# Block 1's mixer computed with the matrix memory before the retention, and RWKV's two directions stepped alternately

## The chip, the cores and the metric

The kernel runs on one core of a Trainium2 chip. The metric is the device time of one execution in microseconds (us), the median of several runs. The profile is one further execution; its span is counted from the first to the last recorded instruction.

## What is computed

Two transformer blocks follow each other on a sequence of 256 tokens of width 1024. Block 1 sees 16 learned meta tokens ahead of it (272 rows):

```python
proj = einsum('bnd,dk->bnk', rmsnorm(h), w_in)          # 4112 columns
rq, rk, rv, rg, mq, mk, mv, mo, gate_pre = split(proj)  # eight of 512, one of 16
ret = retention(rotary(rq), rotary(rk), rv)             # forward + backward, 4 heads
y_ret = head_norm(ret, ret_gn_g) * silu(rg)
mq, mk = split(silu(conv5([mq, mk])))
hm = mlstm(mq, mk, mv, gates(gate_pre))                 # forward + backward, 4 heads
y_m = head_norm(sigmoid(mo) * hm, mlstm_gn_g)
h = h + concat([y_ret, y_m]) @ w_out
h = h + expert_choice_ffn(h)                            # 16 experts, capacity 34
...
```

Block 2 mixes the 256 tokens with a context of 256 more by two branches, a gated delta rule (4 heads) and RWKV-7 (8 heads, forward and backward, `S_t = S_{t-1} (diag(w_t) + a_t b_t^T) + v_t k_t^T`), merges both, and ends with 32 small experts in groups. All of it is float32.

## The kernel before, in words

One class, `Net`, builds three stages in one program. The framework below it orders the instructions of every engine itself, once, when the kernel is built: each engine then runs its own list in that order and waits by semaphores. The order of the Python statements gives the priorities, so a block that is written earlier tends to come earlier, and where buffers or banks are missing it comes later.

**`head`** (0 to about 293 us) is block 1's mixer up to the router. `head_body` (L401) loads the rows, norms and transposes them (`uT`), and multiplies by `w_in` in groups of 256 columns. `wgroup` (L378) loads one group (1 MB) into a slot of a ring of weight slots and splits it into two halves of reduced mantissa: the high part by ACT (`wp`, L289), the low part by DVE (`wp`, L290), two instructions of each for a group. `product3` (L299) makes a float32 product of three matmuls (high by high, high by low, low by high). `projT` (L451) gives a 128-column block transposed (`pj`, 24 matmuls), `projN` (L494) a group in token rows (`pn`), with the 16 meta rows by `metas` (L389; `pM`, L395). PSUM has banks under tags: `pa` three, `pc` two, `pm` two, `pb` one.

The parts stand in this order: retention's `rq` and `rk` with rotation (L457 to L475), its decayed scores `rs` times `strip` into `pret` (L484, L485), its values `rv` by `projN(1024)`, its sums `ro` and their head norm (L518 to L525), then the matrix memory: `mq` and `mk` with the convolution (`cv`, L543 and L546), the gates, `mv` by `projN(3072)`, per head the scores (`ms` L616, `pm`) and the sums `mo` (L639), each sum followed by a small chain over ACT and DVE (`rc` L642 to L644, `y` L646 and L647). Then `mo`'s projection (`projN(3584)`), the product with it on POOL (L659) and the head norm (L729 to L733), retention's gate (`pj`, then three ACT instructions L304 to L306 for a sigmoid, then `gate`, L671), and the transposes `trb` of `y` (L680) into `yT`: columns 0 to 3 are retention's (`gate` L684, split by ACT L289 and DVE L290), 4 to 7 the matrix memory's (ACT L688, DVE L689). POOL copies the meta columns of `yT` to `um` (L690). With `um` and `yT` the output product starts: `pM` (L395) and `wo` (L299), four groups of `w_out`. Between the projections `step()` (L427) issues pieces of block 2's adaptive norm (`ada`, L1037), 24 weight loads of 1 MB with 8 matmuls each, through the same ring.

**`ffn`** (about 293 to 1670 us) streams block 1's 16 experts (three matrices of 1024 x 2816) through the same ring of slots (loads by L241 and L283 on SP's queue); the context's part of block 2's mixer runs beside them. Each expert's second product is done one expert later.

**`lat`** (from 1670 us) is block 2 for the 256 tokens. `rwkv` (L1415) works on four pairs of heads, `j` = 0 to 3. For each pair and direction `d`: `rwkv_front` (L1600) builds the triangular matrices (`rmt`, L1628), `rwkv_back` (L1639) inverts them (`r0i…` and `r1i…`, L1164 and L1192, 32x32 and 128x128 matmuls), and then walks over four chunks; each walks through `rp` (L1661, L1676, L1683, L1691) and the state `rSU` (DVE and ACT at L1680, DVE at L1688, POOL `rsw` at L1672). These are generators: a helper `run` drives one to its end. While direction 0 runs, `hop` (through `fill`, L1118) puts pieces of waiting work behind its matmuls: projections `pc` (L1102), the delta rule (`gic`, `gib`, `gp`), the next pair's preparation. `rwkv_out` (L1707) merges the two directions. Direction 0 uses PSUM tag `pa`, direction 1 `pc`, two banks each. After the mixer come its merge and the 32 experts (from about 2140 us).

Of the kernel before, what the change touches and what calls it, by code (L numbers as in the profile page):

```python
# [16 lines left out]
P = 128  # L17
# [145 lines left out]
class Net:  # L163
# [237 lines left out]
    def head_body(self, W):  # L401
# [9 lines left out]
        wq = self.wgroup(w_in, 0)  # L411
# [30 lines left out]
        for hh in range(4):  # L442
            s = rvt(hh, f"strip{hh}")[:, :416] if hh < 3 else W.tile([P, 416], F32, name="strip3", tag="mv0", padded_shape=[P, 516])
# [13 lines left out]
        rqk = []  # L457
        for g in range(2):
            dst = W.tile([P, 4, NTOK], F32, name="qk", bufs=4)
            scale = (P ** -0.5) if g == 0 else 1.0  # L460
            for j in range(4):
                if j % 2 == 0:
                    w = wq if g + j == 0 else self.wgroup(w_in, 512 * g + 128 * j)
                    if g:
                        step(g)
                pj = projT(w, j % 2)
                raw = W.tile([P, NTOK], F32, name="raw", tag="raw", padded_shape=[P, NTOK + 4], bufs=3)
                nc.scalar.activation(raw, pj, AF.Copy, scale=scale)
                tmp = W.tile([P, NTOK], F32, name="rtmp", tag="rtmp", bufs=2)
                for i in (0, 64):  # L470
                    a, c = slice(i, i + 64), slice(64 - i, 128 - i)
                    nc.vector.scalar_tensor_tensor(tmp[a], pj[c], scale, self.ht("sin")[c], op0=ALU.mult, op1=ALU.mult)
                nc.gpsimd.tensor_mul(dst[:, j, :], raw, self.ht("cos"))
                nc.vector.tensor_add(dst[:, j, :], dst[:, j, :], tmp)
            rqk.append(dst)  # L475

        big = W.tile([P, 4, 3, NTOK], F32, name="pret", tag="big")
        prets = [big[:, hh] for hh in range(4)]
        self.ptag = "pc"
        for hh in range(4):  # L480
            pret = prets[hh]
            for t, (n0, n) in enumerate(TT):
                b = self.bank("rs")
                nc.tensor.matmul(b[:n, :NTOK], rqk[1][:, hh, n0:n0 + n], rqk[0][:, hh, :], start=True, stop=True)  # L484
                nc.vector.tensor_mul(pret[:n, t, :], b[:n, :NTOK], strip[hh][:n, 144 - n0:416 - n0])  # L485
# [3 lines left out]
        rv = [rvt(t, f"rv{t}") for t in range(3)]  # L489
# [24 lines left out]

        projN(1024, out_rv)


        self.ptag = "pc"  # L518
        for t, (n0, n) in enumerate(TT):
            ro = self.bank("ro")  # L520
            for hh in range(4):
                for m, (m0, mn) in enumerate(TT):
                    nc.tensor.matmul(ro[:n, hh * P:(hh + 1) * P], prets[hh][:mn, m, n0:n0 + n],
                                     rv[m][:mn, hh * P:(hh + 1) * P], start=(m == 0), stop=(m == 2))
            self.head_norm(W, y[:n, t, 0:512], ro[:n], n, f"r{t}")  # L525


        self.ptag = "pa"
        mqk = []
        for g in range(2):  # L530
            dst = W.tile([P, 4, NTOK], F32, name="qk", bufs=4)
            for j in range(4):
                if j % 2 == 0:
                    w = self.wgroup(w_in, 2048 + g * 512 + 128 * j)
                    step(1)
                pj = projT(w, j % 2)
                pad = W.tile([P, NTOK + 4], F32, name="pad", tag="raw", bufs=3)
                nc.gpsimd.memset(pad[:, 0:2], 0.0)
# [876 lines left out]
    def rwkv(self, W, F, uT, S, lat, load, tags, start=None):  # L1415
# [92 lines left out]
        for j in range(4):  # L1508
# [8 lines left out]
            for d in range(2):  # L1517
                ys.append(run(self.rwkv_back(j, d, x, fr[d], env)))
# [764 lines left out]
```

## Time and profile before

| what | value |
|---|---|
| runs, us | 2493.68, 2490.26, 2485.04 (median 2490.26) |
| profiled execution, us | 2486.04 |
| its span, us | 2484.3 |
| mean granted TensorE clock (share of full speed) | 0.965 |
| PE busy / DVE / ACT / POOL, us | 2306.2 / 990.8 / 656.0 / 350.8 |
| bytes moved by DMA, mean rate | 755.06 MB, 304 GB/s |

PE is TensorE, PEld its weight loads, DVE VectorE, ACT ScalarE, POOL GpSimd, SP the engine whose queue issues most DMAs. The span contains the three stages one after the other; an engine's share over the span therefore mixes stages with different limits, and the tables by stretches show each of them. [...]

### The profile page before, as it was taken

What the parts mean: (1) busy time and instruction counts of PE and PEld (TensorE: products, weight loads), DVE (VectorE), ACT (ScalarE), POOL (GpSimd) and SP (SyncE); (2) the same over time, 40 slices, a digit from 0 to 9 for tenths busy, and PEclk for the clock granted to TensorE, in tenths of its full rate; (3) what the DMA queues carried; (4) which work ended last, traced back from release to release, by engine and by line L of the source; (5) the groups of instructions that cost most, each with busy time, mean ns of one, the idle gap of its engine ahead of it and who ended that gap; (6) DMA issues with size and microseconds to landing.
All of it is one profiled execution on the core that took longest, in us unless ns stands there. A gap on an engine that the chain in (4) does not pass through costs nothing. (4 is left out here: it accounts for less than half of the span.)

```text
span 2484.3 us, 45165 instructions
## 1 busy us (share of the span) xinstructions
PE 2306.2 (93%) x18736; PEld 1252.2 (50%) x18736; DVE 990.8 (40%) x2419; ACT 656.0 (26%) x1652; POOL 350.8 (14%) x627
## 2 busy tenths in 40 slices
PE   7997799999999999899999998978998999989997
PEld 6765433444444434333433333327777777865554
DVE  6655311323332133223133133216566563645545
ACT  4443111211211222111122121114534332522221
POOL 3101100000001111101011011004243231300000
PEclk9998899999999999999999999998997889999999
DMA  7664999999999999999999999992311113689995
GB/s 244 225 233 132 336 407 402 402 407 405 400 407 398 361 402 405 406 408 406 406 400 406 406 406 406 408 354 67 88 37 38 45 27 95 224 278 365 367 367 182
DMA packets 318816, 755.06 MB, mean 304 GB/s; under 512 B 12944, under 2 KB 158016, under 8 KB 315536
## 3 DMA queue, kind: packets, MB, share of 16 engines
q1 hardware_dynamic: 317104, 747.67, 80.3%
q0 software_dynamic: 1504, 4.46, 0.6%
q8 instruction: 150, 2.46, 0.4%
q14 instruction: 58, 0.48, 0.1%
HBM read 751.03 MB, written 1.05 MB: 303 GB/s over the span
## 5 line engine op out<-in xcount | busy, mean ns | idle before, releaser
L901 PE MATMUL gu<-w,xs 128*64 128x512 f32 (+1 forms) x3072 | 677.2, 568 | 24.3 <-DMA w<-in_w_up 17.2
L901 PEld LDWEIGHTS gu<-w,xs 128*64 128x64 f32 x3072 | 197.5, 137 | 325.2 <-issue 258.0
L933 PE MATMUL dn<-w,hT 128*64 128x512 f32 x1408 | 338.1, 604 | 17.0 <-DMA w<-in_w_down 16.9
L1102 PE MATMUL pc<-luT,w 128*128 128x256 f32 x688 | 177.5, 398 | 1.8 <-DMA w<-in_w_in 1.8
L933 PEld LDWEIGHTS dn<-w,hT 128*64 128x64 f32 x1408 | 88.4, 136 | 171.7 <-issue 116.7
L1102 PEld LDWEIGHTS pc<-luT,w 128*128 128x128 f32 x688 | 126.6, 195 | 19.2 <-DMA w<-in_w_in 2.0
L2139 PE MATMUL egu<-w,exs 128*64 128x256 f32 x1024 | 123.2, 383 | 0.0
L2139 PEld LDWEIGHTS egu<-w,exs 128*64 128x64 f32 x1024 | 74.6, 136 | 39.4 <-issue 6.9
L1672 POOL TENSOR_SCALAR rsw<-rSU,rwc 64x64 f32<-64x64 f32 x112 | 37.2, 332 | 389.3 <-DVE rSU L1688 379.0
L911 DVE TENSOR_TENSOR hid<-hid,gu 128x512 f32<-128x512 f32 (+1 forms) x48 | 30.8, 642 | 130.8 <-ACT hid L306 130.7
L912 DVE TENSOR_TENSOR hid<-hid,gu 128x512 f32<-128x512 f32 (+1 forms) x48 | 30.8, 642 | 119.3 <-PE gu L901 119.2
L1102 PE MATMUL pc<-cuT,w 128*128 128x256 f32 x288 | 71.1, 391 | 0.0
L304 ACT ACTIVATE hid<-gu 128x512 f32<-128x512 f32 (+1 forms) x48 | 26.9, 561 | 160.9 <-PE gu L901 160.7
L2166 PE MATMUL edn<-w,ehT 128*64 128x512 f32 x256 | 67.7, 597 | 0.7 <-ACT ehT L321 0.5
L1102 PEld LDWEIGHTS pc<-cuT,w 128*128 128x128 f32 x288 | 52.0, 189 | 30.8 <-issue 20.4
L1680 DVE COPY rSU<-rp 64x64 f32<-64x64 f32 x64 | 13.8, 215 | 133.0 <-PE rp L1676 132.7
L1628 PE MATMUL rmt<-rT,rBK 128*128 128x128 f32 (+1 forms) x256 | 54.4, 355 | 13.1 <-DVE rT L1615 6.2
L289 ACT CAST wp<-w 128x1024 fp32r<-128x1024 f32 (+1 forms) x48 | 55.1, 1188 | 40.3 <-DMA w<-in_w_in 22.6
L299 PE MATMUL pj<-uTh,wp 128*128 128x272 f32 x320 | 64.8, 296 | 0.0
L290 DVE TENSOR_TENSOR wp<-w,wp 128x1024 fp32r<-128x1024 f32 (+1 forms) x44 | 57.2, 1323 | 15.0 <-ACT wp L289 15.0
L1185 DVE TENSOR_TENSOR r0iB<-r0iB,r0ic 128x128 f32<-128x128 f32 x48 | 13.7, 285 | 114.2 <-PE r0ic L1164 107.4
L2182 DVE TENSOR_TENSOR acc<-acc,esc 128x512 f32<-128x512 f32 x64 | 41.0, 682 | 42.5 <-PE esc L2181 42.5
(675 smaller groups left out, 3560.1 us busy)
## 6 DMA issues: line engine op xcount, KB each, us to landing
w<-in_w_down SPq DMA_DIRECT2D x176, 1024.0 KB, 16.8
w<-in_w_gate SPq DMA_DIRECT2D x128, 1024.0 KB, 17.7
w<-in_w_up SPq DMA_DIRECT2D x128, 1024.0 KB, 17.5
w<-in_w_gate SPq DMA_DIRECT2D x64, 768.0 KB, 16.1
w<-in_w_up SPq DMA_DIRECT2D x64, 768.0 KB, 14.8
w<-in_moe_w_gate SPq DMA_DIRECT2D x32, 1024.0 KB, 13.2
w<-in_moe_w_up SPq DMA_DIRECT2D x32, 1024.0 KB, 12.2
w<-in_moe_w_down SPq DMA_DIRECT2D x32, 1024.0 KB, 11.3
```

Of the source, the lines that this page charges most:

```text
L289: self.nc.scalar.copy(hi, src)
L290: (eng or self.nc.vector).tensor_sub(lo, src, hi)
L299: self.nc.tensor.matmul(out, a[x], b[y], start=(i == 0 and x + y == 0), stop=(i == n - 1 and x == 1))
L901: ins = nc.tensor.matmul(b[h * 64:(h + 1) * 64, :w], xs[:, k, :], ws(k, slice(h * w, (h + 1) * w)), start=(k == 0), stop=(k == KD - 1))
L911: nc.vector.tensor_mul(hid, hid, gu[0][:, :w])
L933: ins = nc.tensor.matmul(dn[0][dc * 64:(dc + 1) * 64], hT[:, j, h * 64:(h + 1) * 64], wd(h * nf + j, slice(dc * 512, (dc + 1) * 512)), sta ...
L1102: self.nc.tensor.matmul(b, w(k), uT[:, k, :], start=(k == 0), stop=(k == KD - 1))
L1628: ins = nc.tensor.matmul(b[:, i], BK[:, c0 + i, h:h + 2, :], T[:, h, c0 + i, :, :], start=True, stop=True)
L1672: nc.gpsimd.tensor_scalar(sw[r], SU[r, h, c, :], wc[r, c:c + 1], 0.0, op0=ALU.mult, op1=ALU.add)
L2139: nc.tensor.matmul(b[64 * i:64 * i + 64, x * 256:x * 256 + 256], xs[:, k, i, :], w[i](k), start=(k == 0), stop=(k == KD - 1))
L2166: nc.tensor.matmul(b[64 * i:64 * i + 64, :], hT[:, j, 64 * i:64 * i + 64], wd[i](j, cs), start=(j == 0), stop=(j == 1))
L2182: nc.vector.tensor_add(h[:, t, cs], h[:, t, cs], b)
```

## The change

Three edits. In `head_body` the matrix memory's projection, gates, values, scores and sums now stand first, then retention's, then `mo`'s projection, the head norm of the matrix memory and retention's gate. The first weight group is that of `mq`; the fourth `strip` has a buffer of its own, and the tiles `rv`, which share buffers with the first three strips, are taken after the scores `pret`. The eight column blocks of `y` are transposed in the order 4 to 7, 0 to 3. In `rwkv` the two directions' `rwkv_back` are driven by `in_turn`, one step of each in turn, where they were driven one after the other; the fills still hang on direction 0 alone.

```diff
-        wq = self.wgroup(w_in, 0)
+        wq = self.wgroup(w_in, 2048)
...
-            s = rvt(hh, f"strip{hh}")[:, :416] if hh < 3 else W.tile([P, 416], F32, name="strip3", tag="mv0", padded_shape=[P, 516])
+            s = rvt(hh, f"strip{hh}")[:, :416] if hh < 3 else W.tile([P, 416], F32, name="strip3")
...
-        rqk = []
-        for g in range(2):
...
-                    w = wq if g + j == 0 else self.wgroup(w_in, 512 * g + 128 * j)
-                    if g:
-                        step(g)
...
-                nc.vector.tensor_mul(pret[:n, t, :], b[:n, :NTOK], strip[hh][:n, 144 - n0:416 - n0])
...
-        projN(1024, out_rv)
...
-            self.head_norm(W, y[:n, t, 0:512], ro[:n], n, f"r{t}")
...
         mqk = []
...
-                    w = self.wgroup(w_in, 2048 + g * 512 + 128 * j)
-                    step(1)
+                    w = wq if g + j == 0 else self.wgroup(w_in, 2048 + g * 512 + 128 * j)
+                    if g:
+                        step(1)
...
         sums(3, pm)
+        self.ptag = "pa"
+        rqk = []
+        for g in range(2):
...
+                    w = self.wgroup(w_in, 512 * g + 128 * j)
+                    step(1)
...
+                nc.vector.tensor_mul(pret[:n, t, :], b[:n, :NTOK], strip[hh][:n, 144 - n0:416 - n0])
+
+        rv.extend(rvt(t, f"rv{t}") for t in range(3))
+        projN(1024, out_rv)
...
+            self.head_norm(W, y[:n, t, 0:512], ro[:n], n, f"r{t}")
...
         mo = [rvt(t, f"mo{t}") for t in range(3)]
         projN(3584, out_mo)
...
-        for k in range(KD):
+        for k in (4, 5, 6, 7, 0, 1, 2, 3):
             b = self.bank("trb")
...
-            ys = []
-            for d in range(2):
-                ys.append(run(self.rwkv_back(j, d, x, fr[d], env)))
+            ys = self.in_turn(tags, [self.rwkv_back(j, d, x, fr[d], env) for d in range(2)])
...
+    def in_turn(self, tags, gens):
+
+        out = [None] * len(gens)
+        todo = list(range(len(gens)))
+        while todo:
+            for i in list(todo):
+                self.ptag = tags[i]
+                try:
+                    next(gens[i])
+                except StopIteration as end:
+                    out[i] = end.value
+                    todo.remove(i)
+        return out
```

What the framework makes of it is seen in the engines' lists. **PE, the last sums of the matrix memory** (`mo<-mv,pm`; `trb<-ctab,y` are the transposes of `y`, `pM` and `wo` the output product). Before, they are the last thing ahead of the transposes and the output:

```order
L639 MATMUL mo<-mv_568,pm_1644 128x129
L639 MATMUL mo<-mv_568,pm_1648 128x129
L680 MATMUL trb<-ctab,y 128x16 x3
L680 MATMUL trb<-ctab,y 128x128 x6
L680 MATMUL trb<-ctab,y 128x16
L680 MATMUL trb<-ctab,y 128x128 x2
L395 MATMUL pM<-w,um 32x256 x8
L299 MATMUL wo<-wp,yT_2124 128x256 x2
```

Now, retention's scores (`rs`) and its value projection (`pn`) come behind them:

```order
L597 MATMUL mo<-mv_584,pm_1010 128x129
L597 MATMUL mo<-mv_584,pm_1014 128x129
L641 MATMUL rs<-qk 16x272
L641 MATMUL rs<-qk 128x272 x2
L641 MATMUL rs<-qk 16x272
L641 MATMUL rs<-qk 128x272
L299 MATMUL pn<-wp,uTh 128x256 x2
L299 MATMUL pn<-wp,uTl 128x256
```

The twelve sums each of the last two heads stand directly ahead of these, with nothing but one small `pM` among them. The line numbers of the changed file are other ones: L597 is the sum, L641 the score, L682 the transpose.

**DVE, the end of the head** (`gate<-pj` is the product behind the last sigmoid, `wp<-w` the split of `w_out`, `hM<-hM,pM` belongs to the output product already). Before:

```order
L729 BN_STATS hnst<-y 128x6 x4
L730 BN_AGGR hnmv<-hnst 128x2 x4
L729 BN_STATS hnst<-y 128x6 x4
L730 BN_AGGR hnmv<-hnst 128x2
L733 TENSOR_SCALAR y<-y,hnmv 128x128 x4
L730 BN_AGGR hnmv<-hnst 128x2 x3
L733 TENSOR_SCALAR y<-y,hnmv 128x128 x4
L689 SCALAR_TENSOR_TENSOR yT_2125<-trb,pcol,yT_2124 128x272 x4
L713 TENSOR_TENSOR hM<-hM,pM 16x256
```

Now:

```order
L735 TENSOR_SCALAR y<-y,hnmv 128x128 x4
L673 SCALAR_TENSOR_TENSOR gate<-pj,pcol,gate 128x272
L691 SCALAR_TENSOR_TENSOR yT_2125<-trb,pcol,yT_2124 128x272 x3
L686 TENSOR_TENSOR gate<-trb,gate 128x272 x2
L290 TENSOR_TENSOR wp<-w,wp 128x1024
L686 TENSOR_TENSOR gate<-trb,gate 128x272 x2
L290 TENSOR_TENSOR wp<-w,wp 128x1024
L691 SCALAR_TENSOR_TENSOR yT_2125<-trb,pcol,yT_2124 128x272
L290 TENSOR_TENSOR yT_2125<-gate,yT_2124 128x272 x4
L323 COPY arow<-ada 128x256
L290 TENSOR_TENSOR wp<-w,wp 128x1024
```

The head norm (`hnst`, `hnmv`, `y`) stands ahead of the last gate now, and behind that gate come products, splits and two of `w_out`'s low parts. On SP's queue the first load of `w_out`, which stood ahead of the load of `hM` and of the last two `ada` loads, now stands behind `hM` and the first of these two; the other three loads of `w_out` stay last.

**PE, the second chunk's step of the first pair** (`rp` is the recurrence; `rT_11729` belongs to direction 0, `rT_11730` to direction 1; `r1ic` is the inversion of direction 1, `rbw` the next pair's preparation). Before:

```order
L1661 MATMUL rp_12623<-rSU_12108,rT_11729 64x64 x2
L1164 MATMUL r1ic<-r1iB 32x32 x16
L1567 MATMUL rbw<-rlo_11679,rlora 128x256
L1567 MATMUL rbw<-rlo_11680,rlora 128x256
L1668 MATMUL rp_12623<-rSU_12108,rT_11729 64x64 x2
L1676 MATMUL rp_12634<-rP_12627,rY_12199 64x64 x2
L1164 MATMUL r1ic<-r1iZ,r1iB 32x32 x16
L1691 MATMUL rp_12623<-rSU_12108,rMR_12118 64x64
L1567 MATMUL rbw<-rlo_11679,rlora 128x256
L1567 MATMUL rbw<-rlo_11680,rlora 128x256
L1683 MATMUL rp_12634<-rSU_12108,rKt_12117 64x64 x2
L1691 MATMUL rp_12623<-rSU_12108,rMR_12118 64x64
```

Now:

```order
L1682 MATMUL rp_12819<-rSU_12108,rT_11729 64x64 x2
L1690 MATMUL rp_12838<-rP_12831,rY_12199 64x64 x2
L1675 MATMUL rp_12828<-rSU_12154,rT_11730 64x64 x2
L1705 MATMUL rp_12819<-rSU_12108,rMR_12118 64x64
L1682 MATMUL rp_12828<-rSU_12154,rT_11730 64x64 x2
L1690 MATMUL rp_12849<-rP_12842,rY_12235 64x64 x2
L1705 MATMUL rp_12828<-rSU_12154,rMR_12164 64x64
L1697 MATMUL rp_12838<-rSU_12108,rKt_12117 64x64 x2
L1705 MATMUL rp_12819<-rSU_12108,rMR_12118 64x64
L1675 MATMUL rp_12866<-rSU_12108,rT_11729 64x64 x2
L1697 MATMUL rp_12849<-rSU_12154,rKt_12163 64x64 x2
L1705 MATMUL rp_12828<-rSU_12154,rMR_12164 64x64
```

Direction 1's inversion, which stood between direction 0's matmuls, is finished before the first step, and its own steps stand there in its place.

## Rows read from the trace of the kernel before

**Rows 1.** The page, the span in 40 equal slices: busy tenths of the DMA engines.

```profile
DMA  7664999999999999999999999992311113689995
```

**Rows 2.** SP's queue, 0 to 330 us: loads waiting for a ring slot (total, times, longest).

```profile
SPq L241 <- PE pM L395: 40.1, 4, 29.7
```

**Rows 3.** The head in stretches of 10 us: busy time (x instructions) by engine, clock, DMA.

```profile
200.00:210.00 10.00, 8.18 (x54) 4.85 (x53) 6.79 (x19) 4.66 (x11) 1.10 (x2) 0.99 0.66 211
210.00:220.00 10.00, 4.70 (x16) 3.72 (x16) 5.83 (x22) 3.65 (x12) 3.36 (x4) 0.50 0.06 7
220.00:230.00 10.00, 3.33 (x16) 2.11 (x20) 7.28 (x33) 2.98 (x9) 1.93 (x3) 0.50 0.00 0
230.00:240.00 10.00, 10.00 (x82) 7.66 (x82) 1.25 (x3) 1.20 (x2) 0.00 (x0) 0.82 0.32 105
```

**Rows 4.** PE's timeline, 196 to 236 us: start, length, instructions, idle time before them.

```profile
207.24 2.40 PE L639 MATMUL mo<-mv,pm 16*128 16x129 f32 x16 [0.82 <-DVE y L647]
...
214.16 4.70 PE L639 MATMUL mo<-mv,pm 16*128 16x129 f32 x16 [4.51 <-DVE rc L643]
...
223.82 0.90 PE L680 MATMUL trb<-ctab,y 128*128 128x128 f32 x3 [2.89 <-DVE y L733]
...
229.87 1.94 PE L395 MATMUL pM<-w,um 128*32 128x256 f32 x16 [1.65 <-POOL um L690]
```

**Rows 5.** ACT's groups by line, 0 to 290 us: busy us, mean ns of one, idle before.

```profile
L646 ACT ACTIVATE y<-mo,rc 128x128 f32<-128x128 f32 (+1 forms) x12 | 4.3, 357 | 3.6 <-DVE rc L644 3.5
...
L305 ACT ACTIVATE gate<-gate,prow 128x272 f32<-128x272 f32 x4 | 2.1, 522 | 0.1
L306 ACT ACTIVATE gate<-gate 128x272 f32<-128x272 f32 x4 | 1.7, 423 | 0.0
...
L304 ACT ACTIVATE gate<-pj 128x272 f32<-128x272 f32 x4 | 1.6, 398 | 5.5 <-PE pj L299 5.5
```

**Rows 6.** DVE's groups by line, 0 to 290 us.

```profile
L290 DVE TENSOR_TENSOR wp<-w,wp 128x1024 fp32r<-128x1024 f32 x40 | 48.2, 1226 | 14.2 <-ACT wp L289 14.1
...
L647 DVE SCALAR_TENSOR_TENSOR y<-mo,rc,y 128x128 f32<-128x128 f32 (+1 forms) x12 | 4.0, 337 | 4.6 <-ACT y L646 4.1 <-ACT rc L642 0.4
...
L643 DVE TENSOR_TENSOR rc<-rc,gcol 128x2 f32<-128x2 f32 (+1 forms) x12 | 2.0, 176 | 3.2 <-ACT rc L642 3.2
L671 DVE SCALAR_TENSOR_TENSOR gate<-pj,pcol,gate 128x272 f32<-128x272 f32 x4 | 2.0, 500 | 2.1 <-ACT gate L306 2.1
...
L689 DVE SCALAR_TENSOR_TENSOR yT<-trb,pcol,yT 128x272 fp32r<-128x272 f32 x4 | 1.8, 498 | 1.1 <-ACT yT L688 1.1
L644 DVE RECIPROCAL rc<-rc 128x2 f32<-128x2 f32 (+1 forms) x12 | 1.8, 156 | 0.2
L684 DVE TENSOR_TENSOR gate<-trb,gate 128x272 f32<-128x272 f32 x4 | 1.7, 436 | 0.2 <-PE trb L680 0.2
...
L290 DVE TENSOR_TENSOR yT<-gate,yT 128x272 fp32r<-128x272 f32 x4 | 1.7, 422 | 0.5 <-ACT yT L289 0.5
```

**Rows 7.** PE's groups by line, 0 to 290 us.

```profile
L1037 PE MATMUL ada<-w,adas 128*32 128x512 f32 x192 | 28.2, 602 | 0.0
```

**Rows 8.** SP's timeline, 130 to 260 us: issue of the first w_out load.

```profile
183.53 0.38 SPq L383 DMA_DIRECT2D w<-in_w_out  x1
```

**Rows 9.** ACT's timeline, 160 to 212 us: the first cast of w_out.

```profile
189.78 1.99 ACT L289 CAST wp<-w 128x1024 fp32r<-128x1024 f32 x2 [0.90 <-DMA w<-in_w_out]
```

**Rows 10.** The latent mixer: whole, then three stretches of 10 us.

```profile
1709.00:2106.00 397.00, 363.57 (x5037) 288.27 (x5036) 237.08 (x680) 159.20 (x497) 133.91 (x240) 0.89 0.18 49
...
1790.00:1800.00 10.00, 4.68 (x91) 3.19 (x78) 9.56 (x22) 7.58 (x24) 6.26 (x7) 0.85 0.06 16
...
1890.00:1900.00 10.00, 9.13 (x61) 7.80 (x62) 7.71 (x22) 4.25 (x13) 4.99 (x11) 0.53 0.01 4
...
1910.00:1920.00 10.00, 10.00 (x212) 8.16 (x210) 2.62 (x9) 2.85 (x10) 2.07 (x6) 0.50 0.20 56
```

**Rows 11.** PE's waits in the latent mixer, 1700 to 2110 us (total, times, longest).

```profile
PE rp L1661 <- DVE rSU L1688: 11.1, 6, 4.3
```

More of the change, by code (lines that the diff above doesn't have):

```diff
@@ L455, in projT @@
             return b
-        rqk = []
+        self.ptag = "pa"
+        mqk = []
         for g in range(2):
             dst = W.tile([P, 4, NTOK], F32, name="qk", bufs=4)
-            scale = (P ** -0.5) if g == 0 else 1.0
             for j in range(4):
                 if j % 2 == 0:
-                    w = wq if g + j == 0 else self.wgroup(w_in, 512 * g + 128 * j)
+                    w = wq if g + j == 0 else self.wgroup(w_in, 2048 + g * 512 + 128 * j)
                     if g:
-                        step(g)
+                        step(1)
@@ L466, in head_body @@
                 pj = projT(w, j % 2)
[L467 to L484, printed above, removed]
-                nc.vector.tensor_mul(pret[:n, t, :], b[:n, :NTOK], strip[hh][:n, 144 - n0:416 - n0])
+                pad = W.tile([P, NTOK + 4], F32, name="pad", tag="raw", bufs=3)
@@ new lines, in head_body @@
+                nc.gpsimd.memset(pad[:, 0:2], 0.0)
+                nc.gpsimd.memset(pad[:, NTOK + 2:], 0.0)
+                nc.scalar.copy(pad[:, 2:NTOK + 2], pj)
+                c = 4 * g + j
+                tmp = W.tile([P, NTOK], F32, name="cv", tag="rtmp", bufs=2)
+                nc.vector.tensor_scalar(tmp, pad[:, 0:NTOK], self.pc("conv_w", c * 5), self.pc("conv_b", c),
+                                        op0=ALU.mult, op1=ALU.add)
+                for k in range(1, 5):
+                    nc.vector.scalar_tensor_tensor(tmp, pad[:, k:k + NTOK], self.pc("conv_w", c * 5 + k), tmp,
+                                                   op0=ALU.mult, op1=ALU.add)
@@ L488, in head_body @@
+                self.sigmoid(dst[:, j, :], tmp)
+                nc.gpsimd.tensor_mul(dst[:, j, :], dst[:, j, :], tmp)
+            mqk.append(dst)
         self.y = y = self.pers.tile([P, 3, D], F32, name="y", tag="tok")
-        rv = [rvt(t, f"rv{t}") for t in range(3)]
+        rv = []
         mv = [W.tile([P, 4, 129], F32, name=f"mv{t}") for t in range(3)]
```

57 lines of the change are left out of this document (30 added, 27 removed).

## The prediction

> **What bounds the kernel now.** I read the page's forty slices first, and there the DMA row [rows 1]. From the fifth to the twenty-seventh slice the DMA engines are at nine tenths or more: block 1's experts are bound by their weights. So are the last experts, in the slices from about 2230 us on. Between them lies a stretch with hardly any DMA, the latent mixer, and ahead of the first lies the head. Both stages that the change touches stand in front of a stream of weights, so what they gain or lose moves the stream as a whole. The waits of SP's queue bear this out at the head's end [rows 2]: the first expert loads wait four times, the longest for 29.7 us, for a ring slot that the matmuls `pM` on `w_out` free. Nothing streams in meanwhile: the DMA share is 0.06 and 0.00 from 210 to 230 us [rows 3]. The head's end is therefore the moment at which `pM` and `wo` begin. I call the idle time before it the bubble.
>
> **The bubble of before.** The table of stretches [rows 3] has PE busy 8.18, 4.70 and 3.33 us in the three tens from 200 to 230 us, which leaves 13.8 us idle. [...] From 230 to 240 us the clock is 0.82, 1.8 us more. The bubble costs 13.8 + 4.0 + 1.8 = 19.6 us. The timeline [rows 4] says what it is made of: the last sums of the matrix memory wait 4.51 us for `rc`, which stands on DVE behind two low parts of `w_out`; the transposes wait for the head norm's `y`, `pM` waits 1.65 us for `um`. Sixteen sums take 2.40 us ahead of the long wait and 4.70 behind it.
>
> **What the change does to the head.** The work is the same: no matmul, load or DVE instruction is added, so only idle time and clock can move.
>
> *The new end.* The last sums, their chain and the matrix memory's head norm now lie ahead of retention's gate and its 24-matmul projections. After the last projection comes a sigmoid on ACT, 0.398 + 0.522 + 0.423 = 1.34 us [rows 5], then DVE's list in the order shown above: `gate` 0.50, four `yT` of the matrix memory 4 x 0.498 = 1.99, four products 4 x 0.436 = 1.74, two low parts of `w_out` 2 x 1.226 = 2.45, four low parts of `yT` 4 x 0.422 = 1.69 [rows 6]. That is 8.4 us. For `um` I add 1 us: in [rows 4] 1.65 us were waited for it, of which one `yT` is 0.5. The end is 10.7 us long. Beside it PE has 24 transposes, which take 0.45 us per three at full clock (half of the 0.90 of [rows 4]), so 3.6 us, and twelve `ada` matmuls of 28.2 / 192 = 0.147 us [rows 7], 1.8 us. Idle: 10.7 - 5.4 = 5.3 us, and I add 1 for the clock. Bounds: zero, if DVE has done most of its list beside the projections; 12.6, if the first load of `w_out` comes late too. That load is now issued behind one more `ada` load. Before, it was issued at 183.53 us [rows 8] and cast from 189.78 [rows 9], 6.3 us later and long before `wo`; I take that cover as still there and cost the move at nothing, and if it is gone, at 6.3.
>
> *The new middle.* The sums of the last two heads now come back to back: six tiles through two PSUM banks. A tile frees its bank when its chain is done: sums 2.40 / 4 = 0.60 us [rows 4], then the reciprocal and the two scalings, 0.176 + 0.156 + 0.337 on DVE [rows 6] and 0.357 on ACT [rows 5], 1.6 us with no hop counted. `rs` follows in the same two banks, and the value projection `pn` behind it cannot pass, since PE takes its list in order. On DVE two pairs of low parts stand among these chains, 4 x 1.226 = 4.9 us. The nearest row is the 4.51 us that one such pair cost before [rows 4]; with two pairs I expect nearly twice this, 8 us, and 2 us of clock behind it. Bounds: 4.5 (one pair is hidden) and 16 (both at 4.5, three rounds of 1.6 for the chain, 2 of clock).
>
> The sum for the head: 19.6 - 6.3 - 10 = **3.3 us gained**; by the ends 15 gained (19.6 - 4.5) and 9 lost (19.6 - 12.6 - 16). The fourth `strip`'s own buffer, the other first weight group and the order of the transposes cost nothing by themselves; the last puts the half that is ready first, and its effect is in the list above.
>
> **What the change does to RWKV.** In the mixer, 1709 to 2106 us, PE is busy 363.6 of 397 us and its mean clock is 0.89 [rows 10]: 33 us idle, and about 0.11 x 397 = 44 us of clock. The instructions are again the same, and filling work remains behind the last pair in both versions, so a shorter chain for direction 1 is worth only the idle time it removes. PE waits six times, 11.1 us, for `rSU` of a chunk's step [rows 11]. With the two directions in turn one wait serves both chains: half of it, 5.5 us. I add 2 for a little of the clock, where the half speed follows such waits (0.53 at 1890 us). Against it: direction 1's inversion no longer stands between direction 0's steps, as the third pair of lists shows. Where DVE is full with the next pair's preparation, PE is busy 4.68 of 10 us even with that cover (1790 us, DVE 9.56) [rows 10]. Another 5.3 us idle for each of the three pairs that have a next one would be 16 us. These ends, 16 lost and 33 gained, are far apart; I take **7.5 us gained**, near the row of the six waits, since both chains now end together and the delta rule's inversions fill between most steps.
>
> [...] From 1910 to 1920 us PE is busy 10.00 of 10 us and yet granted 0.50 [rows 10]. [...]
>
> **Sum.** 3.3 + 7.5 = 10.8 us. The profiled execution took 2486.04 us, so its counterpart takes 2475. It lies 4.2 us below the median of the three runs, 2490.26, so I forecast a median of **2479 us**. About 0.3%, 7.5 us, is what a measurement of this kernel tells from no change.
>
> **The rivals.**
> 1. *Forecast* (0.47): the end gains, the middle gives back half of it, the mixer gains some. 2479, by itself 2470 to 2488.
> 2. *The stall moves, nothing is gained* (0.22). The middle costs 13 us, still under its upper bound, and takes all that the end gives (19.6 - 6.3), and the mixer's filling was as good already. For it: PE is busy 364 of 397 us there, and DVE's list has the low parts of weights between the sums' chains again, as at the end before [rows 4]. Against it: the six waits on `rSU`, which the pairing touches. 2490, 2484 to 2496. The variant that the lists are changed but the waits are the same belongs here.
> 3. *Slower: the paired steps lie bare* (0.21). Two chains that wait at the same time leave nothing between, and the next pair's front cannot begin while direction 1 still walks, as it did before. Price: the 16 us above, less 3 for the head and with 3 for a clock that drops behind the gaps: 2490 + 16 = 2506. It decides if PE's idle time in the mixer rises from 33 to over 45 us.
> 4. *The clock stays up* (0.10). If the waits behind which it fell at 1890 us go, half of the 44 us of clock comes back beside the 10.8: 2490 - 33 = 2457.
>
> **How the numbers follow.** The range leaves out the outer half of the third and fourth case: 2458 to 2505. Faster by over 0.3% (below 2483): seven tenths of the first case, all of the fourth and a little of the second, 0.33 + 0.10 + 0.03 = 0.46. Slower (above 2498): nearly all of the third and a few hundredths from the second's upper end, 0.22. Within: 0.32. Faster and slower are both open; the forecast's own range is 2470 to 2488.
>
> **What would show it.** In the changed profile: no stretch near the head's end at clock 0.50 with PE below half, and `pM` waiting at most 6 us in all behind the last gate; a new wait of PE on `rc` or `pret` in the middle of the head, 5 to 10 us, with low parts ahead of it on DVE; the first expert load some 3 us earlier than now; in the mixer, `rp` of both directions in pairs, PE's idle time about 26 us, and the six waits on `rSU` fewer. The prediction is wrong if the middle costs more than 16 us, if the mixer's idle time grows, or if the streams' start moves without the end of the kernel moving with it.

## The result, and the profile after

The changed kernel takes 2465.4 us (median of 4 runs, 2461.25 to 2467.81) against 2489.46 us of before (4 runs, 2485.04 to 2493.68): a ratio of 0.9895, 95% interval 0.9879 to 0.9911. That is 24 us faster, in the direction of the forecast and inside its range, and more than twice the 10.8 us of its sum. The profiled execution took 2467.81 us, its span is 2466.0 (before 2484.3), its mean clock 0.965, the same as before.

**The head.** The first expert load, in SP's timeline before and after:

```profile
231.87 15.30 SPq L241 DMA_DIRECT2D w<-in_w_gate  x3
```

```profile
227.04 15.32 SPq L241 DMA_DIRECT2D w<-in_w_gate  x3
```

It is issued 4.8 us earlier in this pair of profiles. Over all the profiles of the table below the gain is smaller: the load is issued between 229.7 and 231.9 us (mean 230.9) in the four profiles without any edit of the head, and between 227.0 and 230.4 us (mean 228.6) in the twelve with the head's edits, 2.3 us earlier. The bubble of [rows 3] is gone from the end and has come back smaller in two places. The table of stretches of the changed kernel (columns as in [rows 3]):

```profile
130.00:140.00 10.00, 6.28 (x37) 3.43 (x37) 4.52 (x13) 3.27 (x8) 1.09 (x2) 1.00 0.98 319
140.00:150.00 10.00, 7.45 (x27) 4.54 (x25) 4.27 (x13) 3.37 (x8) 0.00 (x0) 0.51 0.01 3
150.00:160.00 10.00, 10.00 (x51) 7.27 (x52) 3.93 (x10) 0.37 (x1) 0.00 (x0) 0.81 0.00 0
210.00:220.00 10.00, 9.52 (x65) 5.09 (x64) 7.30 (x27) 6.36 (x18) 0.00 (x0) 1.00 1.04 368
220.00:230.00 10.00, 6.92 (x48) 4.33 (x49) 8.56 (x14) 5.94 (x11) 0.46 (x1) 0.83 0.81 252
```

In the middle PE is idle 3.7 and 2.6 us in two neighbouring tens, and its clock is 0.51 in the second and 0.81 in the ten behind them; at the end it is idle 0.5 and 3.1 us at clocks of 1.00 and 0.83. Its timeline names the waits, with the columns of [rows 4]:

```profile
139.87 4.09 PE L597 MATMUL mo<-mv,pm 16*16 16x129 f32 x16 [3.72 <-DVE y L605]
...
145.98 2.38 PE L597 MATMUL mo<-mv,pm 16*128 16x129 f32 x8 [2.03 <-DVE y L605]
...
224.88 0.44 PE L1028 MATMUL ada<-ctab,arow 128*128 128x128 f32 x2 [2.11 <-DVE arow L323]
225.24 1.76 PE L395 MATMUL pM<-w,um 128*32 128x256 f32 x16
```

The sums wait for `y`, the last step of their chains, where they waited for `rc` at the end before; at the end PE waits for `arow`, the copy of the adaptive norm's row, and `pM` no longer waits at all.

**The mixer.** From its first transpose (`afT` of the tokens) to the first matmul of the merge (`mo`) the same 5372 matmul records stand. (A float32 matmul of the program stands in the trace as two records, as the added ones of e5 show, 258 records for 129 matmuls; the counts of the rows are records.) The stretch before and after (columns as in [rows 10]):

```profile
1679.61:2140.38 460.77, 425.64 (x5372) 343.16 (x5373) 264.73 (x741) 194.66 (x588) 148.40 (x278) 0.90 0.22 60
```

```profile
1676.79:2120.72 443.93, 406.89 (x5373) 332.51 (x5373) 259.13 (x741) 193.91 (x588) 149.68 (x278) 0.90 0.22 62
```

It is 16.8 us shorter, 460.8 to 443.9. It starts 2.8 us earlier and so ends 19.7 us earlier; the end of the kernel comes 18.3 us earlier. But PE's idle time did not fall: 460.8 - 425.6 = 35 us outside its matmuls before, 443.9 - 406.9 = 37 after. The clock is 0.90 in both. What fell is the time in which PE is busy, with the same matmuls. The stretch that answers to [rows 10] is as busy as before and holds 98 records more:

```profile
1709.00:2106.00 397.00, 362.62 (x5135) 293.79 (x5136) 236.96 (x688) 165.52 (x507) 132.32 (x235) 0.89 0.22 61
```

The waits for the state did shrink, but others grew by as much. Before, beside the line of [rows 11] (columns as there):

```profile
PE rp L1691 <- DVE rSU L1680: 2.7, 3, 1.3
...
PE r1ic L1164 <- DVE r1iB L1185: 0.3, 1, 0.3
```

After:

```profile
PE rp L1705 <- DVE rSU L1694: 5.9, 6, 2.3
PE rp L1675 <- DVE rSU L1702: 5.4, 4, 2.1
...
PE r1ic L1166 <- DVE r1iB L1187: 3.5, 1, 3.5
```

The six waits of a step's first matmuls fell from 11.1 to 5.4 us (four of them), those of its last matmuls rose from 2.7 to 5.9: 2.5 us less for the state in sum. One wait of direction 1's inversion rose from 0.3 to 3.5 us and took that back.

**What became cheaper.** Two places in PE's timeline of the kernel before, with equal work ahead of the second row of each:

```profile
2101.05 1.89 PE L1102 MATMUL pc<-luT,w 128*128 128x256 f32 x8
2102.88 0.68 PE L1727 MATMUL ryt<-ctab,rys 64*64 64x64 f32 x16
...
2104.26 1.89 PE L1102 MATMUL pc<-luT,w 128*128 128x256 f32 x8
2105.99 0.59 PE L1732 MATMUL rgb<-rsg,rg 128*128 128x256 f32 x2
```

Eight records `pc` of 128x256, in tiles of 128x128, occupy 1.83 us up to the next matmul if that works in tiles of 64x64 (`ryt`), and 1.73 if it has their own shape (`rgb`). Over the mixer's records the same shows as a fixed time: a 128x256 matmul is followed after 216 ns by one of its own shape and after 309 ns by a 32x32 one; a 32x32 matmul is followed by its like after 7 ns and by one of 128x128 after 121 ns (medians at full clock, the same in both kernels). The change costs something once more behind it: the first 128x256 record behind a change is followed by its own shape after 320 ns instead of 216 (median again). So the way out of the large tiles costs 93 ns, the way back some 0.1 us, and the first large matmul there another 104: about 0.3 us for two changes, 0.15 for one. In the mixer the list of before has 446 such changes and the list after has 342. Adding up every interval across a change and the one behind it, less the mean of its like at the same clock, gives 68 us before and 53 after, so 15 of the 16.8 us. What TensorE does in these 93, 114 and 104 ns no run here shows.

### The profile page after: what moved, and what is told of

The parts are those of the page before. It is cut to its first block, busy times and chain, and to the rows that moved or that the text cites. A ratio compares the mean times of both kernels' runs of the same rounds, so it can differ in the third digit from the quotient of the medians.

```text
span 2466.0 us, 45172 instructions
## 1 busy us (share of the span) xinstructions
PE 2288.3 (93%) x18736; PEld 1241.2 (50%) x18736; DVE 981.3 (40%) x2419; ACT 653.4 (26%) x1652; POOL 354.1 (14%) x627
## 5 line engine op out<-in xcount | busy, mean ns | idle before, releaser
L2196 DVE TENSOR_TENSOR acc<-acc,esc 128x512 f32<-128x512 f32 x64 | 41.0, 683 | 42.5 <-PE esc L2195 42.4
```

The lines of the kernel that those rows point to most:

```text
L2196: nc.vector.tensor_add(h[:, t, cs], h[:, t, cs], b)
```

## The experiments

Each mixer below runs from `afT` to `mo`. "Changes" are neighbours in PE's timeline there whose tile shapes differ; "idle" is PE's gaps, each counted from the end of the matmul before it, with the one ahead of the first `afT`, which lies before the stretch and is 8.5 to 8.6 us long in every profile (the stretch less its busy time is smaller by that much); "half clock" is the time there with a granted clock of 0.50.

| profile | changes | idle, us | half clock, us | mixer, us | first expert load, us | ratio to before (95%) |
|---|---|---|---|---|---|---|
| before | 446 | 43.7 | 90.1 | 460.8 | 231.9 | |
| before again (e12) | 446 | 42.7 | 113.1 | 466.8 | 229.7 | |
| change | 342 | 45.6 | 91.5 | 443.9 | 227.0 | 0.9895 (0.9879 to 0.9911) |
| change again (e9) | 342 | 44.5 | 78.2 | 437.9 | 228.7 | 0.9868 (0.9853 to 0.9884) |
| RWKV alone (e1) | 342 | 51.5 | 56.2 | 438.4 | 230.9 | 0.9904 (0.9878 to 0.993) |
| head alone (e2) | 418 | 42.4 | 74.8 | 446.8 | 228.8 | 0.9911 (0.9881 to 0.994) |
| head alone again (e14) | 418 | 42.7 | 74.7 | 447.2 | 228.8 | 0.9911 (0.9895 to 0.9928) |
| inversions in turn (e3) | 352 | 48.8 | 87.1 | 448.7 | 228.1 | 0.9927 (0.9899 to 0.9955) |
| steps in turn (e4) | 425 | 53.0 | 94.0 | 466.2 | 227.9 | 1.0019 (1.0007 to 1.0031) |
| pieces split (e5) | 559 | 48.0 | 101.4 | 497.3 | 230.2 | 1.0152 (1.0123 to 1.0181) |
| pieces joined (e6) | 429 | 45.8 | 64.9 | 464.3 | 228.3 | 1.0059 (1.0035 to 1.0083) |
| fills on second (e7) | 325 | 47.4 | 73.6 | 438.3 | 230.4 | 0.9898 (0.9872 to 0.9924) |
| larger fills (e8) | 315 | 57.0 | 81.3 | 447.3 | 228.6 | 0.993 (0.9902 to 0.9957) |
| fewest shapes (e10) | 281 | 57.7 | 112.8 | 456.2 | 228.3 | 0.9946 (0.9933 to 0.996) |
| before, lumped (e11) | 400 | 46.7 | 70.8 | 449.4 | 231.0 | 0.9949 (0.9934 to 0.9963) |
| transposes only (e13) | 433 | 42.0 | 106.0 | 458.3 | 234.0 | 0.9968 (0.9954 to 0.9982) |
| low parts on POOL (e15) | 343 | 48.3 | 69.2 | 441.3 | 227.6 | 0.9883 (0.986 to 0.9905) |

A least-squares fit over the seventeen rows gives: mixer - idle = 315 + 0.154 x changes + 0.344 x half clock (and 14 more for the two kernels with added matmuls). The errors of the two slopes are 0.007 and 0.022, and no row lies more than 2.2 us off; without the two kernels with added matmuls the slopes are 0.156 and 0.351. The comparisons below use the first two prices. Each row is one profile, and the two rows of before and of the change show how far half clock moves between profiles of one kernel (23 and 13 us).

**e1, RWKV alone.** `rwkv_back` through `in_turn`, `head_body` as before.

```diff
-                ys.append(run(self.rwkv_back(j, d, x, fr[d], env)))
+            ys = self.in_turn(tags, [self.rwkv_back(j, d, x, fr[d], env) for d in range(2)])
```

> RWKV's two directions in turn, block 1's mixer as before. Theory of tile shapes: PE pays about 0.1 us each time the tile shape changes from one matmul to the next (in both traces a 128x256 matmul is followed after 216 ns by one of its own shape and after 309 ns by a 32x32 one; from 32x32 to 128x128 it takes 121 ns instead of 7). PE's list of the latent mixer has 446 such changes in the kernel before and 342 in this one: 104 fewer at 0.11 to 0.15 us, so 12 to 16 us faster than before, with PE's idle time in the mixer unchanged (30 to 34 us). Theory of shared waits (the prediction's): at most 7.5 us faster, and by less idle time. Theory that neither edit does it alone: below 5 us.

Measured: 2464.18 us against 2490.12, 26 us faster, the whole of the gain by itself. The changes account for 104 x 0.154 = 16 us, as the theory of shapes had it; the rest comes with a half clock of 56 instead of 90 to 113 us (12 to 20 us), against 8 us more idle time, where the theory of shapes had expected none. The theory of shared waits falls: idle time rose.

**e2 and e14, the head alone.** The head's edits, with RWKV's directions one after the other.

```diff
-            ys = self.in_turn(tags, [self.rwkv_back(j, d, x, fr[d], env) for d in range(2)])
+            ys = []
+            for d in range(2):
+                ys.append(run(self.rwkv_back(j, d, x, fr[d], env)))
```

> Block 1's mixer with the matrix memory first (and the transposes in the new order), RWKV's directions one after the other as before. The first expert load comes 4 to 6 us earlier than the 231.9 us of before, by every theory. Theory of tile shapes: the list of the latent mixer, which the scheduler orders again, happens to have 418 changes of shape instead of 446, worth 3 to 4 us more: 7 to 10 us faster in all. Theory of shared waits, or that the head's gain is lost on the way to the end: 3 to 5 us faster, or nothing.

> The head's edits alone once more, for a second profile. If the mixer's part at half clock (74.8 us, against 90 and 113 in two profiles of before) belongs to its list, it is again below 85 us and the mixer 444 to 450 us long; if it was chance, the mixer is 450 to 458 us long. The first expert load again 3 us earlier than before.

Measured: 2466.69 against 2490.12 us, and again 2469.29 against 2489.84: 21 to 23 us, two to three times what even the theory of shapes expected. The first load comes at 228.8 us both times, 1 to 3 us earlier than in the two profiles of before and not the 4 to 6 expected by every theory. The mixer, in which no line was edited, is 14 us shorter than in the first profile of before, and so again:

```profile
1675.90:2122.70 446.80, 412.96 (x5371) 334.23 (x5372) 262.51 (x742) 195.82 (x589) 150.83 (x279) 0.92 0.23 65
```

```profile
1675.80:2123.10 447.30, 413.13 (x5373) 334.28 (x5373) 262.51 (x742) 196.28 (x589) 150.52 (x279) 0.92 0.23 65
```

The two profiles agree within 0.5 us in length and 0.1 in half clock, as expected if this mixer belongs to its list. Two profiles are little for that: the two of before, and the two of the change, lie 6 us apart with one list each. The scheduler orders the whole program, and an edit in the head gave the mixer another list: 28 changes less (4 us), and a half clock of 75 us where before has 90 and 113 (5 to 13 us).

**e3 and e4, which half of the pairing.** In both a mark is yielded behind the inversion; in e3 the inversions go in turn and then the steps one direction after the other, in e4 the inversions one after the other and then the steps in turn.

```diff
+        yield 'inverted'
...
+            while todo:
+                for i in list(todo):
+                    self.ptag = tags[i]
+                    if next(gens[i]) == 'inverted':
+                        todo.remove(i)
...
+                ys.append(run(gens[d]))
```

> The whole change, but only the two inversions in turn; the chunks' steps of direction 1 come after those of direction 0. Theory of tile shapes: 352 changes of shape in the mixer's list (342 in the whole change): 1 to 2 us behind the whole change, so 21 to 24 us faster than before. Theory of shared waits: the steps no longer share their waits for the state, so the gain in the mixer is gone: 5 to 9 us faster than before, the head's part alone.

> The whole change, but the two inversions one after the other and only the chunks' steps in turn. Theory of tile shapes: 425 changes of shape in the mixer's list, 83 more than in the whole change at 0.11 to 0.15 us: 9 to 12 us of its gain are lost, so 12 to 15 us faster than before. Theory of shared waits: the steps are what matters, 20 to 24 us faster.

Measured: 2470.86 and 2493.07 us against 2490.12, 19 us faster and 3 us slower. Seen from before, the inversions in turn keep most of the gain, as the theory of shapes expected from 352 changes. But the kernel that differs from both by the pairing alone is e2, at 2466.69 us, and e3 is no faster than that: its 66 changes less (10 us) are taken back by 6.4 us of idle time and 12.3 us of half clock (4 us). So behind the head's edits, pairing the inversions alone gains nothing. The steps in turn alone, on which the forecast had laid all its gain in the mixer, are 26 us slower than e2 and lose even the head's part: their mixer is 22.3 us longer than the change's. Of this 83 x 0.154 = 13 us are changes, 7.4 idle time and 0.9 half clock; the expectation of 9 to 12 us had left the idle time out. It is not the paired steps that wait: PE's waits for the state are 11.0 us in all (14.2 before), but those of the two inversions are 10.5 us (3.5 before), above all this one, before and in e4:

```profile
PE r1ib L1192 <- DVE r1iZ L1196: 1.3, 2, 0.7
```

```profile
PE r1ib L1194 <- DVE r1iZ L1198: 5.1, 1, 5.1
```

The stretch of e4's mixer:

```profile
1675.50:2141.70 466.20, 421.62 (x5372) 338.00 (x5373) 266.70 (x741) 195.14 (x588) 148.52 (x278) 0.90 0.21 59
```

**e5 and e6, changes of shape added.** 129 small matmuls (258 records) that add zero, apart or together, and nothing else between the two kernels.

```diff
+            for _ in range({1: 1, 3: 1, 5: 1}.get(k, 0) if every == 1 and hasattr(self, "zz") else 0):
+                self.nc.tensor.matmul(b[0:32, 0:32], self.zz[0:32], self.zz[0:32], start=False, stop=False, tile_position=(0, 0))
```

(e6 has `{3: 3}` in place of `{1: 1, 3: 1, 5: 1}`; `zz` is a tile of zeros.)

> The whole change, and in each projection `pc` of the mixer that is issued after RWKV's start (43 of them, 8 matmuls each) three added matmuls of 32x32 on zeros, one each behind the second, fourth and sixth matmul; they add zero to the result. Theory of tile shapes: PE's list of the mixer has 559 changes of shape instead of 342; at 0.11 to 0.18 us each (0.11 is what the gaps between matmuls show at full clock, 0.18 what the mixers of the runs so far show per change in their list) 24 to 39 us slower than the whole change. Theory that the mixer follows idle time and clock alone: the 129 small matmuls cost 1 to 4 us, like those of the next kernel.

> The same 129 added matmuls of 32x32, but all three behind the fourth matmul of the projection, so that they share two changes of shape. Theory of tile shapes: 429 changes of shape in the mixer's list, 9 to 16 us slower than the whole change and 14 to 23 us faster than the kernel with the pieces apart. Theory of idle time and clock: within 4 us of the kernel with the pieces apart.

Measured: 2529.48 and 2502.01 us, 27 us apart for the same matmuls. The two mixers:

```profile
1676.50:2173.90 497.40, 451.70 (x5631) 340.02 (x5631) 255.36 (x744) 193.27 (x592) 149.19 (x279) 0.90 0.19 52
```

```profile
1676.70:2141.00 464.30, 421.83 (x5630) 335.87 (x5630) 260.62 (x743) 193.20 (x592) 147.97 (x279) 0.93 0.20 56
```

They differ by 33.0 us: 2.2 idle, 36.5 x 0.344 = 12.6 for half clock, and 18.2 for 130 changes, 0.14 each. PE's timeline shows it directly, with the pieces apart and joined:

```profile
1760.79 1.13 PE L1104 MATMUL pc<-luT,w 128*128 128x256 f32 x4
1761.85 0.24 PE L1106 MATMUL pc<-zz 32*32 32x32 f32 x2
1762.02 1.13 PE L1104 MATMUL pc<-luT,w 128*128 128x256 f32 x4
1763.08 0.24 PE L1106 MATMUL pc<-zz 32*32 32x32 f32 x2
1763.25 1.13 PE L1104 MATMUL pc<-luT,w 128*128 128x256 f32 x4
```

```profile
1761.72 1.99 PE L1104 MATMUL pc<-luT,w 128*128 128x256 f32 x8
1763.64 0.37 PE L1106 MATMUL pc<-zz 32*32 32x32 f32 x6
1763.94 3.29 PE L1104 MATMUL pc<-luT,w 128*128 128x256 f32 x14
```

Apart, four records of 216 ns (0.86 us) and two small ones repeat every 1.23 us: 0.37 us for two changes and two small records. Joined, eight records (1.73 us at 216 ns) and six small ones take 2.22 us, from 1761.72 to 1763.94: 0.49 us for two changes and six small records. The four small records more cost 0.12 us, 0.03 each; without them both patterns leave 0.31 us for two changes, 0.15 for one, which is the fit's price. The theory of idle time and clock alone falls.

Both kernels came out far slower than expected, seen from the whole change: e5 by 64 us where 24 to 39 were expected, e6 by 37 where 9 to 16 were. The added matmuls cost 14 us by the fit, beyond their changes, where I had expected 1 to 4; and the stretch behind the mixer, which has no added matmul, is 11 us longer in both (356.1 and 356.5 us from the mixer's end to the span's, 345.3 in the change). Why that is so is open.

**e7, e8 and e10, fewer changes.** e7 hangs the fills on direction 1; e8 puts the step's fills in one place; e10 joins e7 with one larger fill behind every second group of an inversion.

```diff
-        hop = (lambda *steps: (lambda ins: self.fill(ins, *steps))) if lat and d == 0 else lambda *steps: (lambda ins: None)
+        hop = (lambda *steps: (lambda ins: self.fill(ins, *steps))) if lat and d == 1 else lambda *steps: (lambda ins: None)
```

```diff
-HOPS = 4, 1, (3, 1), (2, 1), (2, 1), (2, 1), (0, 4), (0, 4)
+HOPS = 4, 1, (3, 1), (4, 2), (0, 0), (0, 0), (0, 4), (0, 4)
```

```diff
-HOPS = 4, 1, (3, 1), (2, 1), (2, 1), (2, 1), (0, 4), (0, 4)
+HOPS = 4, 1, (6, 2), (2, 1), (2, 1), (2, 1), (0, 4), (0, 4)
-            hop(tiled(x, Nm, Ya))
+            tiled(x, Nm, Ya)
```

> The whole change, and in RWKV's back part the fills hang on direction 1's matmuls instead of direction 0's, so that the two directions' matmuls of one kind stand next to each other and the filling work behind both. Theory of tile shapes: 325 changes of shape in the mixer's list instead of 342, 2 to 3 us faster than the whole change. Theory of shared waits or idle time: no faster, and up to 8 us slower, since direction 0 now waits without anything behind it.

> The whole change, and in a chunk's step the fills of three places are put in one place in larger lumps (four and two pieces behind the first matmuls, none behind the two later ones). Theory of tile shapes: 315 changes of shape in the mixer's list instead of 342, 3 to 5 us faster than the whole change. Theory of idle time: the two later places wait bare, 5 to 15 us slower.

> The whole change with the fills behind direction 1, and in the inversions one fill in twice the size behind every second group of 32x32 matmuls instead of one behind each. Theory of tile shapes: 281 changes of shape in the mixer's list instead of 342; 61 x 0.16 us (the slope over the ten mixers measured so far) is 10 us less, so about 2456 us, if idle time (45.6 us) and half clock (91.5 us) stay. Theory of shared waits or of the chain: no faster than the whole change; the inversions' chains wait with less behind them, 5 to 15 us slower.

Measured: 2464.17, 2470.96 and 2477.27 us against 2490.94, 2490.94 and 2490.59. e7 is no faster than the change (0.9898 beside 0.9895 and 0.9868). e8 pays for 27 changes less with 11 us of idle time and is 12 us slower than the change on the same chip (e9, 2458.91), as the theory of idle time had it. e10, with the fewest changes of all, is 18 us slower than e9, and the expectation of 10 us faster was wrong:

```profile
1675.20:2131.40 456.20, 407.05 (x5372) 337.98 (x5373) 260.46 (x742) 193.97 (x589) 149.41 (x279) 0.88 0.23 64
```

```profile
1675.60:2113.60 438.00, 402.10 (x5373) 329.29 (x5373) 258.89 (x741) 194.03 (x588) 149.39 (x278) 0.91 0.23 63
```

Against e9 its changes save 61 x 0.154 = 9 us, its idle time is 13.2 us longer, and its half clock 34.6 us longer, worth 12. The proviso of the expectation, that idle time and clock stay, did not hold. The two inversions of RWKV wait no more than in e9 (6.0 us in all, 7.6 there). New are waits of the delta rule's inversion, 5.6 us that e9 does not have:

```profile
PE gic L1166 <- POOL giB L1181: 3.1, 1, 3.1
PE gic L1166 <- DVE giB L1187: 2.5, 1, 2.5
```

The waits for weights (`pc` for `w_in`) rose from 1.8 to 5.2 us, and those of `rp` from 11.5 to 14.3. Since e8, which leaves the inversions' fills as they are, has 6.4 us of the wait on `giB` too, it is not shown that the missing fills make it.

**e9 and e12, the same kernels again.**

> The whole change once more, for the spread of its profile and for a comparison on the chip of the next kernels. All theories: about 2465 us, 24 us faster than before. If the part of the mixer at half clock (91.5 us in its first profile) belongs to the list of instructions, it comes out within 10 us of that; if it is chance, anywhere from 55 to 100.

> The kernel before once more, for the spread of its profile: 446 changes of shape by every theory, a mixer of about 461 us. If half clock belongs to the list, 80 to 100 us of the mixer at half clock again; if it is chance, anywhere from 55 to 110, and the mixer's length moves by about 0.32 of the difference.

Measured: 2458.91 us for the change (before on that chip 2490.59, so 32 us faster and not 24) and 2492.86 for before, in one run. The half clock moved from 91.5 to 78.2 and from 90.1 to 113.1 us, so a part of it is chance, more than the 10 us by which a list's own was to be known (113.1 lies outside both ranges expected). The mixer of before with it:

```profile
1680.20:2147.00 466.80, 432.63 (x5373) 348.82 (x5373) 264.85 (x741) 195.03 (x588) 147.13 (x278) 0.88 0.21 59
```

It is 6.0 us longer than in the first profile; 23.0 x 0.344 gives 7.9 us more, less 1.0 of idle time.

**e11, before with lumped fills.** e10's last two edits in the kernel before, with none of the change.

> The kernel before, with nothing of the change, and only the inversions' fills lumped (one of twice the size behind every second group). Theory of tile shapes: 400 changes of shape in the mixer's list instead of 446, 46 x 0.16 = 7 us faster than before. Theory of shared waits, or that the order of the two directions is what matters: no gain, 0 to 10 us slower.

Measured: 2476.13 us against 2490.59, 14 us faster. The 46 changes are worth 7.1 us, as expected; half clock, 71 us, gives 7 to 15 more, against 3 to 4 of idle time. A fixed order of the two directions is no condition for the gain.

```profile
1679.70:2129.10 449.40, 411.23 (x5371) 334.60 (x5372) 260.99 (x742) 194.85 (x589) 148.34 (x279) 0.92 0.23 64
```

**e13, the transposes alone.** The order 4 to 7, 0 to 3 in the kernel before.

```diff
-        for k in range(KD):
+        for k in (4, 5, 6, 7, 0, 1, 2, 3):
```

> The kernel before with nothing but the new order of the head's eight transposed column blocks. The head's work stays in its place, but the scheduler orders the mixer's list anew: 433 changes of shape instead of 446. Theory that the head's edit works on the mixer through the list: a head within 2 us of before (first expert load near 231 us), and a mixer of another length, 2 us shorter by the changes of shape and up to 10 us either way by idle time and half clock. Theory that the gain of the head's edit is earned in the head: no difference beyond 3 us anywhere.

Measured: 2480.63 us (10 runs, 2474.06 to 2489.99) against 2489.84. The mixer's list changes to 433 and its mixer is 2.5 us shorter than in the first profile of before, 8.5 than in the second; the first load comes 2 to 4 us later. So an edit in the head does reach the mixer through the list. How much of the 9 us lies there is not settled: the profiled execution, with a span of 2487.1 us, was one of the slowest of these runs.

**e15, low parts on POOL.** What is left of the stall in the head's middle.

```diff
-                w = self.wgroup(w_in, c0 + 256 * c)
+                w = self.wgroup(w_in, c0 + 256 * c, nc.gpsimd if c0 == 1024 else None)
```

(`wgroup` passes this engine on to `split`.)

> The whole change, and the low parts of the two weight groups of retention's values made by GpSimd, which is idle there, instead of by DVE, where they stand ahead of the chains behind the last sums. Theory of the head (the prediction's middle stall is DVE's order): the wait of the sums in the middle of the head, 5.7 us, falls to 3 us or less and the first expert load comes 2 to 4 us earlier than in the whole change. Theory that the two PSUM banks set the stall: no difference there; if GpSimd is too slow for the halves, 1 to 5 us later.

Measured: 2461.34 us, a ratio of 0.9883 that is no different from the change's. The wait of the sums in the head, in PE's waits of the change and of this kernel:

```profile
PE mo L597 <- DVE y L605: 5.7, 2, 3.7
```

```profile
PE mo L597 <- DVE y L605: 4.7, 1, 4.7
```

It fell by 1 us, not by half, and the first load did not move (227.6). These two groups' low parts are not what sets most of the stall; the two PSUM banks were not tried with it.

## Why the prediction was right in sign and wrong in size

- **Both stages stand ahead of a stream, and their gain goes through.** Right: 19.7 us at the mixer's end are 18.3 at the end of the kernel. The head's 4.8 us at the first load are 2.8 at the mixer's start; over the sixteen profiles above they are 2.3 at the first load and 3.8 at the mixer's start (means of 1676.2 and 1680.0).
- **The bubble moves and shrinks.** Right. The end was to cost 6.3 us and cost 3.6 of idle time and, by estimate, 1.7 of clock (0.17 of ten us at 0.83); the middle was to cost 10 and cost 6.3 idle and, by estimate, 4 to 6 of clock (7.5 us of work at 0.51, then ten at 0.81). The sum of the head, 3.3 us, stands beside 4.8 in the first pair of profiles and 2.3 over all of them. Its detail was wrong at two points. PE waits for `arow`, not for `um`. And 2.40 / 4 = 0.60 us is not a tile's sums: the sixteen records are two tiles of eight, 1.2 us each, which makes the chain's round 2.2 us and the upper bound of 16 some 2 us higher.
- **The mixer.** This step failed: "The instructions are again the same, and filling work remains behind the last pair in both versions, so a shorter chain for direction 1 is worth only the idle time it removes." The first half is true and the conclusion does not follow. The time of a list is not the sum of its instructions; here it also has a term for the neighbours. 446 changes of shape against 342 are worth 104 x 0.154 = 16 us, which no step of the prediction contained. The row for it was in the trace of before (1.83 against 1.73 us). By its own sign the forecast failed too: it was to be wrong if the mixer's idle time grew, and in the stretch of [rows 10] it went from 33.4 to 34.4 us instead of to 26.
- **Half of the six waits, 5.5 us.** Wrong in sum: the waits for the state fell by 2.5 us, an inversion's wait took that back, and idle time rose by 2 us. e4, where only the steps are in turn, loses 26 us against e2 (10.6 us of it idle time).
- **The clock, 2 us.** Too small on the average of two profiles each: half clock 101.6 us before, 84.9 after, worth 6 us. In the first two profiles it was nothing (90.1 and 91.5), so that these 6 us may be luck. The price was too high: the prediction counted half of the time at 0.50, 44 us in the mixer, where 0.344 x 90.1 are 31. In the head, the 4.0 us of clock in the bubble's 19.6 are a term that no run shows; what the traces show is that sixteen sums took 4.70 us there and 2.40 ahead of it [rows 4], that three transposes `trb` took 0.90 us at 0.50 and 0.75 at 1.00 (changed kernel, at 214.45 us), and that in the mixer of before a 128x128 record follows its like after 214 ns at 0.50 and 112 at 1.00 (medians).
- **The rivals.** The third did not come for the whole change. e4 has the paired steps and is 28 us slower than the whole change, but its idle time in the stretch of [rows 10] is 38.9 us, under the 45 that were to decide, and it stands at the inversions, not at the steps. The fourth's 33 us are near the 32 of e9, without its mechanism: half clock fell by 17 us on average, not by half.

The sum as measured, first against second profiles averaged: head 3 to 4, changes 16, half clock 6, idle time -2: 23 to 24 us, beside the 24 of the first comparison and the 32 of e9. The two edits do not add up: 26 and 21 to 23 us alone, 24 to 32 together. The changes of shape are the 342 of e1 in the whole change too, and the head's part is there; what each edit alone has besides is a shorter half clock (56 and 75 us, where the two profiles of the change have 92 and 78). Why the whole change does not keep that is not shown.

Open are what makes a list run at half clock, how much of that part is chance, and why e5 and e6 lose 11 us behind the mixer.

## What to carry to other kernels

Count the changes of tile shape in TensorE's order when small-tile matmuls (inversions, recurrences) are mixed with large ones, and price each at what the gaps in the trace show, that of the first matmul behind the change included; put like beside like, but look at the idle time too: e8 and e10, with the fewest changes, lost more by it and by half clock than the changes gave. Where a scheduler orders the whole program, compare the lists of the stages that were not edited too, before a gain is booked to the edit. And profile a kernel twice before a clock difference of some 20 us is read as an effect.

## What was not expected of the hardware

A change of tile shape costs more than one 128x128 record takes (0.15 us beside 112 ns from one such record to the next, median before and after), and a good part of it falls behind the change, on the first large matmul (320 ns instead of 216). This mixer's time at half clock costs 0.34 us per us and not 0.5, which fits that a 128x256 record takes twice as long there (427 ns instead of 216) while a 32x32 one follows its like after 7 ns (medians) at either clock. And the half clock of one and the same kernel moved by 13 and by 23 us between two executions, while that of another agreed within 0.1.
